# Bonus products ahead of substitution steps on VectorE, and a longer hold for the second merging product's PSUM bank in the planned TensorE order

## The chip, the cores and the metric

One core of one Trainium2 chip runs the whole program in one launch. The metric is device time in microseconds (us); lower is better. Engines are named as in the profile: PE is TensorE's matmul, PEld its weight load, DVE is VectorE, ACT is ScalarE, POOL is GpSimd, SP is the queue that issues most transfers.

## The reference, cut to what matters

One layer of a streaming encoder, for 64 frames of a running stream and 512 frames of a new one (576 tokens together), all in fp32:

```python
h = rms_norm(x, g_pre_mix)
p = h @ w_in                       # columns: r | k | v | lora_w | lora_a | lora_g | u | v_gmlp | gate_A | gate_B
# o_A, 16 heads of 64: delta-rule recurrence over the tokens, computed in chunks of 64
S = S * w_t + (S @ a_t) b_t^T + v_t k_t^T;   y_t = S @ r_t
bonus = sum_over_head(r * k_mod * r_k) * v
o_A = (group_norm(y) + bonus) * g
o_B = u * (tril(W_s) @ layer_norm(v_gmlp) + b)
m = sigmoid(gate_A) * (o_A @ w_proj_a) + sigmoid(gate_B) * (o_B @ w_proj_b)
x = x + rms_norm(m @ w_o, g_post_mix)
x = x + rms_norm((silu(f @ w_gate) * (f @ w_up)) @ w_down, g_post_ffn)      # f = rms_norm(x, g_pre_ffn)
```

Returned are both outputs, the shift rows, the recurrence states and the normalised v rows.

## The kernel before, in words

The first half of the time (to about 585 us) computes o_A for eight pairs of heads, one pair after the other, while the big projections `h @ w_in` and the weights' conversion run in between. Every fp32 weight block is split on ACT (`whi`, L302) and POOL (`wlo`, L305) and multiplied as three products; a projection block is 48 products of 128x288 into a bank of its own tag (`pj`, three banks).

For a pair p the work is cut into streams, which are Python generators:

- `elementwise(p)`: small products `z` (from the lora inputs), their tanh `sg` on ACT, a running sum `L` on DVE (L670), its exponentials `EL` (L674) and `EN` (written into `sg`, L676) on ACT, head norms `n`, then the inner products `am` into four banks, and last `bo`, the head sums of r * k * r_k, in two halves. The bonus products of the title, `bonus<-bo,v` at L790 on DVE, read the two `bo` banks and so set them free. The next pair's `elementwise` begins behind them.
- `substitute(p)`: 15 steps of forward substitution on 16x16 blocks, each an `Xt` (L863) and an `X` (L866) on DVE, 80 partitions wide. The first one is pinned behind all that was traced on DVE before it.
- `inverse(p)`: reads the substituted blocks back, and merges them into larger inverses. The first merging product (`m1`), the second (`m2`) and then `mp` and `mu` follow one another; each is many tiny products into one bank, which ACT evicts. In the trace `m1` and `m2` both appear as `m`; the eviction of the second is `IV<-m` at L903, four instructions.
- `turns(p)`: transposes `tb`, with a fifth block in a bank `tr` that three groups share. ACT copies them out to `At` and `Kt` (L818 for `tb`, L819 for `tr`), and DVE copies out the last group; TensorE may write the shared bank again only when its reader is done. POOL writes `AR<-eye` (L822) after the first group.
- `batch(p)`: products `d`, `e`, `c` and `y`; DVE adds the results of `e` and `c` into `TD` and `AR` (L972, L973); `y` takes three banks.
- `chain(p)` (products `pc`, sums `S` at L1011, then `py`) and `finish(p)` (group norm; products `to` and `g`).

All of these small products share four PSUM banks (tag `a`, `ps1`), handed out in turn.

Two mechanisms set the order of instructions. TensorE's is fixed when the program is built: the class `Weave` keeps a clock of its own (`clk.now`), adds an estimate for each matmul, and takes the first stream whose waiting time is over; while none is ready it emits the next piece of a projection. The estimates of waiting times are in the table `LAT`. Of the four banks it knows only how long each is held, which is the second argument of `ps1`:

```python
    def take(self, hold):
        self.banks.sort()
        self.banks.pop(0)
        self.banks.append(self.now + hold)

    def free(self, n=1):
        while sorted(self.banks)[n - 1] > self.now:
            yield sorted(self.banks)[n - 1] - self.now
```

A stream that needs n banks yields on `clk.free(n)`, and the clock fills the time with projections. The inner products `am` ask for four free banks. The holds are numbers in the order only: whether a bank is really free is a semaphore's matter.

The order on the other engines comes from the framework's scheduler, which plans readiness when the program is built and among ready instructions takes the one traced first; each engine then executes in that order. `tc.high_priority(HPO)` ranks an instruction as if it were traced 3000 places earlier. In the kernel before it is used for the shifted inputs (`k<-pj`, L489).

Of the kernel before, what the change touches and what calls it, by code (L numbers as in the profile page):

```python
# [8 lines left out]
ALU = mybir.AluOpType  # L9
# [8 lines left out]
HALF = T // 2  # L18
# [14 lines left out]
HPO = 3000  # L33
# [27 lines left out]
SB = 16  # L61
# [172 lines left out]
def layer(tc, I, O):  # L234
# [3 lines left out]
    pe, dve, act, pool, sp = nc.tensor, nc.vector, nc.scalar, nc.gpsimd, nc.sync  # L238
# [23 lines left out]
    def ps1(name, hold=0.0):  # L262
        clk.take(hold)
        return psum.tile([P, 512], F32, tag="a", bufs=nb["a"], name=name)
# [7 lines left out]
    def mmul(out, lhsT, rhs, **kw):  # L272
        n = 1
        for d in rhs.shape[1:]:
            n *= d
        rows = lhsT.shape[0]
        if rows != clk.rows:
            clk.now += 0.12
            clk.rows = rows
        if rhs.dtype == F32R:  # L280
            clk.now += 0.011 + n / 2400
        elif rows == P:
            clk.now += max(n, P) / 600
        else:
            clk.now += n / 2000 if rows == 64 else 0.037 if rows == 32 else 0.02
        return pe.matmul(out, lhsT, rhs, **kw)  # L286
# [210 lines left out]
    for k in range(KD):  # L497
        t = xp.tile([P, T], F32, name=f"x{k}")
# [101 lines left out]
    for k in range(KD):  # L600
        t = xp.tile([P, T], F32, tag="xsq", bufs=4, name="xn")
# [50 lines left out]
    def elementwise(E):  # L652
# [128 lines left out]
        bonus = rp2.tile([P, T], F32, tag="bonus", bufs=2, name="bonus")  # L781
        yield LAT["bo0"]
        yield (("v", hp_), LAT["v"])
        v = E["v"]
        for hs in HS:
            yield from clk.free()
            sb = ps1("bo", 2.0)
            mmul(sb[:, 0:HALF], bonesr, rkh[:, hs], start=True, stop=False)
            mmul(sb[:, 0:HALF], bonesr, rkl[:, hs], start=False, stop=True)
            dve.tensor_tensor(bonus[:, hs], sb[:, 0:HALF], v[:, hs], ALU.mult)  # L790
            yield LAT["bo"]
        E["bonus"] = bonus
        clk.signal("elem", hp_)
# [77 lines left out]
    def inverse(E):  # L871

        hp_, AB, di = E["hp"], E["AB"], d_inv[E["hp"]]
        yield LAT["O"]
        for h in range(2):
            for b in range(64 // SB):
                r0_ = 64 * h + SB * b
                sp.dma_start(IV[r0_:r0_ + SB, :, SB * b:SB * b + SB], di[1, h, b].rearrange("u s t -> s u t"))
        blocks = [(64 * h, 64 * h + 32) for h in range(2)]
        quarters = [(64 * h + 32 * b, 32 * b) for h in range(2) for b in range(2)]  # L880
        turn = lambda: dve.transpose(IT.rearrange("p c t -> p (c t)"), IV.rearrange("p c t -> p (c t)"))
        U = AB.rearrange("p j h t -> p (j h) t")
        yield lat("U", hp_)
        if hp_ > 0:
            yield (("d", hp_ - 1), 0.0)

        PT = rp.tile([P, 10, SB], F32, tag="PT16", name="PT16")
        tc.keep_in_program_order(turn())
        yield lat("m1", hp_)
        yield from clk.free()  # L890
        pp = ps1("m1", 1.8)[:, 0:10 * SB].rearrange("p (c t) -> p c t", t=SB)
        for u in range(10):
            for r, q in quarters:
                mmul(pp[r:r + 32, u], U[r:r + SB, u, q:q + 32], IT[r:r + SB, u, q:q + SB], start=True, stop=True)
        act.activation(PT, pp, ACT.Copy, scale=low)
        yield lat("m2", hp_)
        yield from clk.free()
        pp = ps1("m2", 2.2)[:, 0:10 * SB].rearrange("p (c t) -> p c t", t=SB)
        for u in range(10):
            for r, q in quarters:  # L900
                mmul(pp[r:r + SB, u], PT[r:r + 32, u, :], IV[r:r + 32, u, q + SB:q + 32], start=True, stop=True)
        for r, q in quarters:
            act.activation(IV[r:r + SB, :, q + SB:q + 32], pp[r:r + SB], ACT.Copy)  # L903

        PT = rp.tile([P, 10, 32], F32, tag="PT", name="PT")
        turn()
        yield lat("mp", hp_)
        yield from clk.free()
        pp = ps1("mp", 1.9)[:, 0:320].rearrange("p (c t) -> p c t", t=32)
        for u in range(10):  # L910
            for a0, a1 in blocks:
                mmul(pp[a1:a1 + 32, u], U[a0:a1, u, 32:64], IT[a0:a1, u, 0:32], start=True, stop=True)
        for _, a1 in blocks:
            act.activation(PT[a1:a1 + 32], pp[a1:a1 + 32], ACT.Copy)
        yield lat("mu", hp_)
        yield from clk.free()
        pp = ps1("mu", 1.9)[:, 0:320].rearrange("p (c t) -> p c t", t=32)
        for u in range(10):
            for _, a1 in blocks:
                mmul(pp[a1:a1 + 32, u], IV[a1:a1 + 32, u, 32:64], PT[a1:a1 + 32, u, :], start=True, stop=True)  # L920
        for _, a1 in blocks:
            act.activation(IT[a1:a1 + 32, :, 0:32], pp[a1:a1 + 32], ACT.Copy)
        clk.signal("it", hp_)
# [147 lines left out]
    def elem_all():  # L1071
        for p_ in range(NPAIR):
            if p_ > 0:
                yield (("elem", p_ - 1), 0.0)
            yield from elementwise(EV[p_])
        sp.dma_start(O["shift"], shc)
        yield (("values", NPAIR - 1), 0.0)
        e_es.close()
        R["g"], R["gp"] = mk("gmlp")
        R["vn"] = [slot(j) for j in range(5)]  # L1080
        clk.signal("vn")
        R["ln"] = [slot(5 + i) for i in range(2)]
        R["tril"] = R["gp"].tile([P, P], F32, name="tril")
        sp.dma_start(R["tril"], I["cst"][:, NCST:])
        for i in range(2):
            sp.dma_start(R["ln"][i][0:64], I["rows"][i:i + 1, :].broadcast_to([64, D]))
# [6 lines left out]
    def inv_all():  # L1093
        for p_ in range(NPAIR):
            yield (("x", p_), 0.0)
            yield from inverse(EV[p_])
# [465 lines left out]
```

## Time and profile before

| | us |
|---|---|
| median of 3 runs | 1229.72 (1229.62 to 1234.26) |
| the profiled execution's own time | 1231.22 |
| its span in the profile | 1229.2 |
| PE busy | 1185.0 (96%) |
| DVE busy | 548.7 (45%) |
| ACT busy | 466.8 (38%) |
| POOL busy | 603.3 (49%) |

A row of a timeline reads: start, length, engine, line, operation, output<-inputs, shapes, count; in square brackets the engine's idle time before it and who ended it. A row of waits reads: who waited, for whom, us in total, times, longest. A row of windows reads: stretch, length, then the busy time of PE, PEld, DVE, ACT and POOL with instruction counts, the granted TensorE clock (1.00 is full speed), the DMA share and GB/s.

### The profile page before, as it was taken

Reading aid. Unit: us, or ns where it says so; the run is one execution under the profiler, and the core shown is the slowest. Engines: PE = TensorE matmul, PEld = TensorE weight load, DVE = VectorE, ACT = ScalarE, POOL = GpSimd, SP = SyncE. Lnnn points to the kernel's source line nnn. Section 1 sums busy time; section 2 is a strip of 40 time slices with the busy share of each in tenths; the row PEclk is TensorE's granted clock in tenths of the full one; section 3 lists DMA queues with packets and bytes.
Section 4 is the critical chain, followed back from the end, with each engine's and each line's share of the span. In section 5 each row is a group of like instructions: output and inputs, shape, how many; then the busy total and the mean of one; then the engine's idle time right before and its main releaser. Section 6 shows DMA issues by size and latency. Waiting matters only on the chain.

```text
span 1229.2 us, 29962 instructions
## 1 busy us (share of the span) xinstructions
PE 1185.0 (96%) x12938; PEld 1152.1 (94%) x12938; DVE 548.7 (45%) x1086; ACT 466.8 (38%) x889; POOL 603.3 (49%) x477
## 2 busy tenths in 40 slices
PE   7999999999999999999999999999999999999997
PEld 6999998989888989899999999999999999999996
DVE  5756556656565656422624431754333333300103
ACT  5555544444444453343431333543222222222220
POOL 6675353535352636242545652465565555634442
PEclk9999999999999999999999999999999999999998
DMA  5233322222212222351744542232222222242222
GB/s 185 80 106 105 91 59 79 62 81 61 81 60 81 61 76 61 97 153 47 230 126 131 179 141 70 77 121 86 86 85 73 85 86 86 79 159 82 80 76 77
DMA packets 68276, 118.05 MB, mean 96 GB/s; under 512 B 30832, under 2 KB 36208, under 8 KB 68144
## 3 DMA queue, kind: packets, MB, share of 16 engines
q1 hardware_dynamic: 68000, 116.06, 30.9%
q8 instruction: 101, 1.65, 0.6%
q14 instruction: 31, 0.25, 0.1%
q10 hardware_dynamic: 144, 0.08, 0.0%
HBM read 99.83 MB, written 16.28 MB: 94 GB/s over the span
## 4 chain that ended last, share of the span: by engine, by line
PE 81%; DVE 11%; ACT 4%; issue 2%; DMA 1%; POOL 1%; POOLq 0%; ACTq 0%; DVEq 0%; SPq 0%
PE fg L286 21%; PE pj L286 17%; PE po L286 15%; PE gv L286 4%; PE pb L286 4%; PE pa L286 3%; PE fp L286 2%; PE z L286 2%; DVE X L866 1%; DVE Xt L863 1%; PE am L286 1%; PE pc L286 1%; DVE TD L972 1%; PE wv L286 1%; PE d L286 1%
## 5 line engine op out<-in xcount | busy, mean ns | idle before, releaser
L305 POOL TENSOR_TENSOR wlo<-raw,whi 128x512 fp32r<-128x512 f32 (+1 forms) x286 | 395.3, 1405 | 346.4 <-ACT whi L302 322.8
L302 ACT ACTIVATE whi<-raw 128x1024 fp32r<-128x1024 f32 x143 | 149.2, 1047 | 280.4 <-PE fg L286 174.6
L1306 DVE TENSOR_TENSOR rs<-rs,nsq 128x288 f32<-128x288 f32 (+2 forms) x12 | 9.1, 755 | 106.0 <-ACT nsq L1305 106.0
L1378 DVE TENSOR_TENSOR ft<-ft,fg 128x288 f32<-128x288 f32 x40 | 16.4, 450 | 68.2 <-PE fg L286 66.7
L1372 DVE TENSOR_TENSOR fg<-fg,rs 128x288 f32<-128x288 f32 x40 | 16.4, 452 | 63.3 <-PE fg L286 63.2
L1375 DVE SCALAR_TENSOR_TENSOR ft<-ft,fg 128x576 f32<-128x576 f32 (+1 forms) x24 | 27.9, 1163 | 18.4 <-ACT ft L1374 18.4
L1376 POOL TENSOR_TENSOR ft<-ft,rs 128x576 f32<-128x576 f32 (+1 forms) x24 | 31.9, 1327 | 6.5 <-DVE ft L1375 5.8
L1042 POOL TENSOR_TENSOR gm<-gm,mhalf 128x10 f32<-128x10 f32 x8 | 15.7, 1957 | 39.0 <-DVE gm L1041 39.0
L866 DVE TENSOR_TENSOR X<-X,Xt 80x15 f32<-80x15 f32 (+7 forms) x120 | 32.3, 269 | 3.9
L863 DVE TENSOR_TENSOR Xt<-X,M 80x15 f32<-80x15 f32 (+7 forms) x120 | 31.3, 261 | 4.9 <-DMA M<-d_inv 1.3
L822 POOL TENSOR_TENSOR AR<-eye,eC 128x576 f32<-128x576 f32 x8 | 9.4, 1177 | 47.3 <-PE tr L290 47.3
L368 POOL TENSOR_TENSOR rr<-rm,mhalf 128x3 f32<-128x3 f32 (+1 forms) x6 | 5.0, 831 | 51.9 <-DVE rm L367 51.9
L702 POOL TENSOR_TENSOR rmul<-cst,rn 128x1280 f32<-128x1280 f32 x8 | 19.0, 2379 | 22.8 <-DVE S L1011 21.0
L1011 DVE TENSOR_TENSOR S<-pc,C 128x64 f32<-128x64 f32 x48 | 10.2, 212 | 44.3 <-PE pc L286 44.3
L286 PE MATMUL pj<-h1h,whi 128*128 128x288 f32 x88 | 29.5, 336 | 0.0
L286 PE MATMUL am<-AR,BK 64*64 64x128 f32 x640 | 23.9, 276 | 4.8 <-ACT IV L903 4.8
L286 PE MATMUL pj<-h3h,whi 128*128 128x288 f32 x88 | 28.5, 324 | 0.0
L286 PE MATMUL pj<-h7h,whi 128*128 128x288 f32 x88 | 28.4, 323 | 0.0
L286 PE MATMUL pj<-h4h,whi 128*128 128x288 f32 x88 | 27.6, 313 | 0.0
L286 PE MATMUL pj<-h5h,whi 128*128 128x288 f32 x88 | 27.6, 313 | 0.0
L286 PE MATMUL pj<-h2h,whi 128*128 128x288 f32 x88 | 27.1, 308 | 0.0
L286 PE MATMUL pj<-h0h,whi 128*128 128x288 f32 x88 | 27.0, 307 | 0.0
(1200 smaller groups left out, 4304.2 us busy)
## 6 DMA issues: line engine op xcount, KB each, us to landing
raw<-in_w_in SPq DMA_DIRECT2D x50, 512.0 KB, 3.7
raw<-in_w_gate SPq DMA_DIRECT2D x22, 512.0 KB, 3.6
raw<-in_w_up SPq DMA_DIRECT2D x22, 512.0 KB, 3.6
raw<-in_w_down SPq DMA_DIRECT2D x16, 512.0 KB, 3.6
raw<-in_w_gv SPq DMA_DIRECT2D x8, 512.0 KB, 3.8
raw<-in_w_proj_a SPq DMA_DIRECT2D x8, 512.0 KB, 3.9
raw<-in_w_proj_b SPq DMA_DIRECT2D x8, 512.0 KB, 3.7
raw<-in_w_o SPq DMA_DIRECT2D x8, 512.0 KB, 3.6
```

What stands on the lines that cost most here:

```text
L286: return pe.matmul(out, lhsT, rhs, **kw)
L302: keep(act.activation(hi[:, :cols], raw[:, :cols], ACT.Copy))
L305: keep(pool.tensor_tensor(lo[:, c0:c1], raw[:, c0:c1], f(hi[:, c0:c1]), ALU.subtract))
L702: pool.tensor_tensor(rmul.rearrange("p j h t -> p (j h) t"), mask.unsqueeze(1).broadcast_to([P, 10, P]), rn.unsqueeze(2).broadcast_to([P, ...
L863: ins = dve.tensor_tensor(t3, X[:, 0:r, s:s + 1].broadcast_to([NU, r, w]), M[:, s:s + 1, s + 1:SB].broadcast_to([NU, r, w]), ALU.mult)
L866: dve.tensor_tensor(X[:, 0:r, s + 1:SB], X[:, 0:r, s + 1:SB], t3, ALU.add)
L972: dve.tensor_tensor(TD[rows, cs, rows], ps[rows, :, 1, :], by_place[rows, cs, 0, :], ALU.add)
L1042: pool.tensor_tensor(m, m, mhalf, ALU.pow)
L1372: keep(dve.tensor_tensor(g[:, HS[h]], pg, rs2[:, HS[h]], ALU.mult))
L1375: keep(dve.scalar_tensor_tensor(t[:, ts], t[:, ts], 1.0, g[:, ts], ALU.add, ALU.mult))
L1376: pool.tensor_tensor(t[:, ts], t[:, ts], rs2[:, ts], ALU.mult)
L1378: dve.tensor_tensor(t[:, HS[h]], t[:, HS[h]], pu, ALU.mult)
```

## The change

Two edits. The two bonus products of each pair are traced under high priority. The hold that the planned TensorE order counts for the bank of the second merging product goes from 2.2 to 3.4 (us of the planner's clock). No instruction is added or removed, and no operand changes.

```diff
@@ elementwise
             sb = ps1("bo", 2.0)
             mmul(sb[:, 0:HALF], bonesr, rkh[:, hs], start=True, stop=False)
             mmul(sb[:, 0:HALF], bonesr, rkl[:, hs], start=False, stop=True)
-            dve.tensor_tensor(bonus[:, hs], sb[:, 0:HALF], v[:, hs], ALU.mult)
+            with tc.high_priority(HPO):
+                dve.tensor_tensor(bonus[:, hs], sb[:, 0:HALF], v[:, hs], ALU.mult)
             yield LAT["bo"]
@@ inverse
-        pp = ps1("m2", 2.2)[:, 0:10 * SB].rearrange("p (c t) -> p c t", t=SB)
+        pp = ps1("m2", 3.4)[:, 0:10 * SB].rearrange("p (c t) -> p c t", t=SB)
         for u in range(10):
             for r, q in quarters:
                 mmul(pp[r:r + SB, u], PT[r:r + 32, u, :], IV[r:r + 32, u, q + SB:q + 32], start=True, stop=True)
```

## The prediction

> **What bounds the kernel now.** I read the page first, then TensorE's waits, then the timeline around the longest ones, then the granted clock by windows.
>
> ```profile
> PE 1185.0 (96%) x12938; PEld 1152.1 (94%) x12938; DVE 548.7 (45%) x1086; ACT 466.8 (38%) x889; POOL 603.3 (49%) x477
> ...
> PE y L286 <- DVE bonus L790: 11.9, 6, 2.3
> PE am L286 <- ACT IV L903: 4.8, 6, 1.1
> ...
> PE tr L290 <- ACT Kt L819: 0.3, 1, 0.3
> ```
>
> TensorE is busy for 96% of the span, and neither edit removes work from it. So the change can only take idle time away, or time at a reduced clock. The other rows are waits of TensorE between 100 and 600 us, the two largest and a small one: six times `y` waits for a bonus product, six times `am` for the eviction L903, once a third transpose for `Kt`. I number the passes 2 to 7 by the pair whose `bo` and X steps run there; `y` then belongs to the pair before.
>
> A wait can cost more than itself:
>
> ```profile
> 213.30:216.70 3.40, 1.77 (x14) 1.53 (x13) 1.17 (x1) 2.14 (x7) 0.20 (x1) 1.00 0.14 29
> 216.70:220.10 3.40, 3.15 (x26) 2.91 (x25) 1.76 (x5) 3.40 (x7) 2.25 (x2) 1.00 0.27 27
> 267.90:271.30 3.40, 3.40 (x55) 3.28 (x48) 2.99 (x15) 1.61 (x6) 0.00 (x0) 0.50 0.39 153
> ...
> 387.30:390.70 3.40, 1.55 (x57) 1.48 (x58) 3.23 (x10) 0.32 (x2) 1.36 (x2) 1.00 0.30 60
> 390.70:394.10 3.40, 3.40 (x15) 3.40 (x15) 2.95 (x15) 2.03 (x8) 0.00 (x0) 0.51 0.24 96
> ...
> 448.70:452.10 3.40, 2.40 (x64) 2.34 (x65) 3.09 (x14) 1.17 (x6) 0.25 (x1) 1.00 0.53 159
> ...
> 510.20:513.60 3.40, 3.40 (x15) 3.40 (x16) 2.50 (x13) 0.99 (x4) 0.00 (x0) 0.50 0.20 81
> ```
>
> After a stretch of 3.4 us with PE busy for 1.55 us (387.30, pass 5), the next 3.4 us are granted half the clock, which costs 1.7 us of work; after 1.77 us busy (213.30, pass 2) they are not. A half-clock stretch followed the `y` wait in four passes, 3, 4, 5 and 7, the first at 267.90 and the last at 510.20; pass 6's wait escaped (448.70). Together the `y` waits cost 11.9 + 4 x 1.7 = 18.7 us. The question is how much of that comes back.
>
> **The change, part by part. The bonus products.** Pass 4, with the end of its stream on each engine:
>
> ```profile
> 320.95 0.85 DVE L972 TENSOR_TENSOR TD<-e,AR 64x256 f32<-64x256 f32 x2
> 322.76 0.16 DVE L863 TENSOR_TENSOR Xt<-X,M 80x15 f32<-80x15 f32 x1
> 323.91 0.29 PE L286 MATMUL bo<-rkl,bonesr 128*128 128x288 f32 x1
> 327.43 0.45 DVE L790 TENSOR_TENSOR bonus<-bo,v 128x288 f32<-128x288 f32 x1
> 327.94 0.55 PE L286 MATMUL y<-Vt,AK 64*64 64x64 f32 x10 [2.28 <-DVE bonus L790]
> 332.14 0.18 DVE L866 TENSOR_TENSOR X<-X,Xt 80x15 f32<-80x15 f32 x1
> 337.03 0.27 PE L290 MATMUL tr<-cst,BK 128*128 128x128 f32 x1
> 354.78 0.84 DVE L881 STREAM_TRANSPOSE IT<-IV 128x640 f32<-128x640 f32 x1 [0.15 <-issue]
> ```
>
> The product at 327.43 stands behind twelve X operations, though both halves of `bo` are done by 324.20. Ranked ahead, it runs about 3.5 us earlier, before `y` needs its bank at 325.66 (327.94 less 2.28). The wait goes. No instruction is added: the two products (0.45 us each) stood inside the X chain anyway, so its end at 332.32 stays. Even later it would not matter for the blocks' way back, which DVE takes up at 354.78. SP's queue keeps its order, and neither product issues a transfer. A product put ahead of an unfinished `bo` would idle DVE: none of that at best; at worst both ahead of the first X, which is 0.9 us per pass net (below, fourth rival). I take none, because `bo`'s first half is done when X begins.
>
> What is late next: the second `tr`, which needs `At` copied out (L819). ACT does that behind `EL` (L674), `EL` needs `L`, and `L` stands behind the X steps on DVE. Pass 2 shows it, because its `y` wait was only 0.78 us:
>
> ```profile
> 202.50 0.16 DVE L863 TENSOR_TENSOR Xt<-X,M 80x15 f32<-80x15 f32 x1
> 206.18 0.55 PE L286 MATMUL y<-Vt,AK 64*64 64x64 f32 x10 [0.78 <-DVE bonus L790]
> 212.02 1.15 POOL L822 TENSOR_TENSOR AR<-eye,eC 128x576 f32<-128x576 f32 x1 [6.54 <-PE tr L290]
> 212.17 1.04 DVE L866 TENSOR_TENSOR X<-X,Xt 80x15 f32<-80x15 f32 x1
> 213.12 1.34 DVE L670 TENSOR_TENSOR_SCAN L<-rmask,sg 128x576 f32<-128x576 f32 x1
> 214.56 0.69 ACT L674 ACTIVATE EL<-L 128x576 f32<-128x576 f32 x1 [2.09 <-DVE L L670]
> 215.15 0.26 ACT L819 ACTIVATE At<-tr 128x128 f32<-128x128 f32 x1
> 215.46 0.33 PE L290 MATMUL tr<-cst,BK 128*128 128x128 f32 x1 [1.63 <-ACT At L819]
> ```
>
> From the first X to the second `tr` pass 2 took 12.96 us, bound by DVE and ACT all along: no gap on DVE before `L`, TensorE waiting at the end. That includes an X step stretched from 0.18 to 1.04 us beside POOL's L822, which in passes 3 to 6 fell after X (TensorE was late) and will fall into it once TensorE is early. So 12.96 us is my floor for passes 2 to 6. What they take now:
>
> ```profile
> 262.22 0.16 DVE L863 TENSOR_TENSOR Xt<-X,M 80x15 f32<-80x15 f32 x1
> 276.39 0.27 PE L290 MATMUL tr<-cst,BK 128*128 128x128 f32 x1
> ...
> 384.22 0.16 DVE L863 TENSOR_TENSOR Xt<-X,M 80x15 f32<-80x15 f32 x1
> 398.17 0.27 PE L290 MATMUL tr<-cst,BK 128*128 128x128 f32 x1
> ...
> 444.52 0.16 DVE L863 TENSOR_TENSOR Xt<-X,M 80x15 f32<-80x15 f32 x1
> 457.16 0.27 PE L290 MATMUL tr<-cst,BK 128*128 128x128 f32 x1
> ```
>
> Pass 3: 14.17; pass 4: 337.03 - 322.76 = 14.27; pass 5: 13.95; pass 6: 12.64. Against the floor that is -1.2, -1.3, -1.0, +0.3, and nothing for pass 2 (its 0.78 us moves to the `tr` wait): -3.2 us. Pass 7 has no `L` behind its X, and `y` is TensorE's only wait there, so it gets all back: -2.3 - 1.7 = -4.0.
>
> The new `tr` waits are long. Pass 2: 1.63 + 0.78 = 2.4. Pass 4: 12.96 - (14.27 - 2.28 - 1.7) = 2.7; 3 and 5 alike. Pass 6: 12.96 - (12.64 - 2.3) = 2.6. By the windows above a wait lowers the clock if about 1.75 us of it falls into one window; for 2.6 us that holds for (1.65 + 0.85) / 3.4 = 0.74 of the positions. The wait of pass 6 that escaped makes me take a little less, 3 of 5 passes: +5.1 us. Bounds: 0 and +8.5.
>
> **The longer hold.**
>
> ```profile
> 360.46 0.82 PE L286 MATMUL m<-IV,PT 32*16 32x16 f32 x80
> 362.19 1.30 PE L286 MATMUL am<-AR,BK 64*64 64x128 f32 x34
> 363.34 1.20 ACT L903 ACTIVATE IV<-m 16x160 f32<-16x160 f32 x4
> 364.59 0.68 PE L286 MATMUL am<-AR,BK 64*64 64x128 f32 x14 [1.10 <-ACT IV L903]
> ```
>
> This is the longest of the six. The bank of `m2` is taken at 360.46 and free at 364.54: 4.1 us, where the order counts 2.2. With 3.4 the order puts 1.2 us more of projections ahead of `am`; it starts at 363.4, its first part needs 1.3 us, and the rest meets a free bank. `am` ends where it did (363.4 + 2.0 against 365.27), so what it feeds, the eight transfers on SP included, does not move on the chip. The projections are done earlier instead of later, at no cost while others are left. Term: -4.8, bounds 0 and -4.8.
>
> The cover for that is the stretch behind the last `py`:
>
> ```profile
> 584.97 0.34 PE L286 MATMUL py<-S,AR 64*64 64x64 f32 x8
> 613.73 0.74 DVE L347 TENSOR_TENSOR m7l<-xt,m7h 128x576 fp32r<-128x576 f32 x1
> 631.87 0.43 PE L286 MATMUL pa<-m7h,whi 128*128 128x288 f32 x2
> ```
>
> The last pair's result is ready (`m7l`, 614.47) 29.5 us after `py`, and TensorE first uses it 46.9 us after. Eight passes that each draw 1.2 us of projections forward shorten that by 9.6 us; 7.8 us are left, so I cost it at nothing. With the cover gone each further us would be one of waiting.
>
> Behind the second `tr` pass 2 also has the small wait of the third for `Kt` (0.3 us in the waits, the only one). It should come to four more passes; I take 0.25 each: +1.0.
>
> Sum: -4.8 - 4.0 - 3.2 + 1.0 + 5.1 = -5.9 us. The profiled execution took 1231.22 us, 1.5 above the median; I take the difference off the median: 1223.8, say 1224 (a profiled execution of 1225.3).
>
> **The rivals.** First, ACT copies `At` ahead of `EL`, so that no `tr` wait follows: all waits and all half-clock stretches go, -4.8 - 18.7 = -23.5, or 1206. For it: the scheduler's plan sees TensorE earlier. Against: in pass 2, with TensorE early, L674 still stands ahead of L819.
>
> Second, the `tr` waits come but leave the clock alone: -11.0, or 1219. For it: pass 2's window with 1.77 us busy, behind a wait of 1.63. Against: the window with 1.55, and waits that are longer. [...]
>
> Third, the priority moves nothing, because the products become ready late in the plan: only the second edit acts, -4.8, or 1225. Against: twelve X operations are passed over with `bo` done.
>
> Fourth, and slower: the products are planned ahead of DVE's sums too, and DVE stands idle for `bo`. If both were ahead of X only, X would start at 324.2 + 0.45 instead of 322.76, 1.9 later, with 0.9 saved inside the chain: 1.0 per pass, five passes, and the gain is just gone. Ahead of the sums from 320.95 on, their 1.9 us come on top: 2.9 x 5 = 14.5, so +8.6, or 1238. It decides from 2.4 us per pass, (5.9 + 6.1) / 5. Against: the product has only `bo` to wait for, and the scheduler ranks it only once it expects `bo` done.
>
> **How the numbers follow.** About 0.5%, 6 us, is what a measurement of this kernel can tell from no change, so "faster" means below 1223.6. My forecast has 0.46, with a range of its own from 1219 to 1228 (two to five half-clock stretches, a floor off by 0.5 us per pass); the rivals have 0.12, 0.20, 0.09 and 0.13. Faster: 0.12 + 0.19 + 0.4 x 0.46 = 0.49. Slower: 0.11, most of the fourth. Same: the rest, 0.40. The range 1206 to 1232 leaves out about half of the first rival and most of the fourth, under 2 in 10.
>
> **What would show it.** Right: no `y` wait on `bonus`, no `am` wait on L903, products right behind `bo` on DVE; in five passes a `tr` wait of 2.4 to 2.8 us on L819, 12.9 to 13.1 us after the first X, half clock after about three of them; pass 7 shorter by 4 us. Wrong: L819 ahead of L674 (first rival), DVE idle for `bo` (fourth), or new waits at `mp`, `gv` or `pa`, since the projections' order moves as a whole.

## The result, and the profile after

The changed kernel took 1248.73 us (median of four runs, 1242.86 to 1251.72), the kernel before on the same chip 1230.03 (1229.62 to 1234.26). The ratio is 1.0138 with a 95% interval of 1.0095 to 1.0182: slower by 1.4%, or 18.7 us by the medians. The forecast was 1224, and its range ended at 1232.

TensorE's waits after (who waited, for whom, us in total, times, longest):

```profile
PE d L286 <- DVE oo L1063: 17.1, 5, 4.6
PE pc L286 <- DVE S L1012: 5.8, 4, 2.0
PE pc L286 <- DVE So L1012: 5.5, 3, 1.8
PE pa L286 <- ACT s L448: 1.9, 1, 1.9
PE y L286 <- DVE bonus L791: 0.2, 1, 0.2
```

Both waits that the forecast wanted gone are gone: `y` for the bonus product fell from 11.9 to 0.2 us, and `am` for the eviction (L903 before, L904 after, where the new line moves the rest down by one) is no longer in the list. In their place stands one that the forecast does not name, 17.1 us at `d` for the product `oo<-oo,g` on VectorE, and 11.3 us at the chain's `pc`. Waits changed by 17.1 + 11.3 - 11.9 - 4.8 = +11.7 us.

The summary of the bonus sums' second products, first for the kernel before, then after, and behind each the first part of the projection through `w_proj_a` (count, shortest/median/longest ns, first and last start in us):

```profile
L286 PE MATMUL bo<-rkl,bonesr x16: 292/294/297, 89.8 to 504.7; 128*128 128x288 f32 x16
L286 PE MATMUL pa<-m0h,whi x16: 293/295/399, 615.1 to 669.1; 128*128 128x288 f32 x16
```

```profile
L286 PE MATMUL bo<-rkl,bonesr x16: 291/296/445, 90.2 to 522.9; 128*128 128x288 f32 x16
L286 PE MATMUL pa<-m0h,whi x16: 293/295/422, 633.8 to 689.4; 128*128 128x288 f32 x16
```

The first `bo` falls at the same time, the last 18.2 us later (504.7 to 522.9), and `pa` begins 18.7 us later. So the whole loss has arisen by the last `bo`, that is in passes 2 to 7, and the stretch behind it is as long as it was. In that stretch the `y` wait and the half clock of pass 7 are gone (4.0 us by the forecast's reading), but `pa` waits 1.9 us where it waited 0.5, and 3.4 us from 617.0 on are granted half the clock (0.51 from 616.9 to 620.3). Windows over most of those passes, before and then after (stretch, length, busy time of PE, PEld, DVE, ACT and POOL with counts, granted clock, DMA share, GB/s):

```profile
200.00:530.00 330.00, 311.44 (x4985) 294.14 (x4976) 199.12 (x477) 150.37 (x345) 142.77 (x114) 0.98 0.26 74
```

```profile
200.00:530.00 330.00, 300.78 (x4834) 283.32 (x4833) 189.96 (x471) 142.85 (x329) 140.99 (x110) 0.96 0.25 69
```

TensorE is idle for 10.7 us more, and the clock is lower by 0.02, which is 6.6 us of 330. Together 17.3 us, near the 18.2. In that stretch eight slots of 3.4 us were granted half the clock (0.50 or 0.51, from 258.6, 262.0, 292.7, 326.8, 347.3, 391.7, 456.6 and 477.1), four before (from 267.8, 329.3, 390.7 and 510.2): 4 x 1.7 = 6.8 us.

Pass 5 of the changed kernel shows the new wait (timeline: start, length, engine, line, operation, in brackets the idle time before it and who ended it; `M` in a row is the tile that the first X step reads, brought by a transfer):

```profile
381.17 0.33 SPq L856 DMA_DIRECT2D M<-d_inv  x1
...
384.14 0.17 DVE L864 TENSOR_TENSOR Xt<-X,M 80x15 f32<-80x15 f32 x1 [5.92 <-DMA M<-d_inv]
384.51 0.29 PE L286 MATMUL g<-dgh,lgl 128*128 128x288 f32 x1
385.54 1.17 PE L286 MATMUL d<-AB,IT 64*64 64x128 f32 x32
388.99 0.75 DVE L1056 TENSOR_TENSOR oo<-oo,bonus 128x576 f32<-128x576 f32 x1
390.81 0.44 DVE L1063 TENSOR_TENSOR oo<-oo,g 128x288 f32<-128x288 f32 x1
391.31 0.75 PE L286 MATMUL d<-AB,IT 64*64 64x128 f32 x4 [4.60 <-DVE oo L1063]
395.55 0.46 DVE L791 TENSOR_TENSOR bonus<-bo,v 128x288 f32<-128x288 f32 x1 [1.12 <-PE bo L286]
```

VectorE reaches the first X step 5.92 us before the transfer of `M` has landed, and everything behind that step waits with it: first the sum `oo<-oo,bonus`, then the products `oo<-oo,g` that free the banks of `g`. TensorE finished `g` by 384.8 and then multiplied 32 of the 36 parts of `d`; the last four need a third bank, `g`'s, and start only at 391.31. In the same pass of the kernel before VectorE did these things in another order:

```profile
374.98 0.76 DVE L1055 TENSOR_TENSOR oo<-oo,bonus 128x576 f32<-128x576 f32 x1 [2.48 <-ACT oo L1053]
378.20 0.46 DVE L1062 TENSOR_TENSOR oo<-oo,g 128x288 f32<-128x288 f32 x1 [2.46 <-PE g L286]
381.20 0.86 DVE L972 TENSOR_TENSOR TD<-e,AR 64x256 f32<-64x256 f32 x2 [1.76 <-PE e L286]
384.22 0.16 DVE L863 TENSOR_TENSOR Xt<-X,M 80x15 f32<-80x15 f32 x1
388.65 0.44 DVE L790 TENSOR_TENSOR bonus<-bo,v 128x288 f32<-128x288 f32 x1
```

There `oo`, then `TD`, then X, and the bonus product within X. After, the bonus product stands behind X, yet not because of a rank: its `bo` is issued only at 395.03. X itself begins at 384.2 in both, but the changed kernel is 8.5 us behind by then (the `py` of this pass starts at 364.82, not 356.34), so X has moved that much nearer to `py` and in front of work that stood ahead of it. VectorE's waits for `M` in the changed kernel (the kernel before has 1.3 us, once):

```profile
DVE Xt L864 <- DMA M<-d_inv: 24.3, 6, 5.9
```

### The profile page after: what moved, and what is told of

It is laid out like the page before. It is cut to its first block, busy times and chain, and to the rows that moved or that the text cites. A ratio compares the mean times of both kernels' runs of the same rounds, so it can differ in the third digit from the quotient of the medians.

```text
span 1241.1 us, 29948 instructions
## 1 busy us (share of the span) xinstructions
PE 1183.5 (95%) x12938; PEld 1150.2 (93%) x12938; DVE 538.1 (43%) x1086; ACT 466.5 (38%) x889; POOL 606.4 (49%) x477
## 4 chain that ended last, share of the span: by engine, by line
PE 70%; DVE 15%; ACT 6%; DMA 4%; issue 2%; SPq 2%; POOL 1%; ACTq 0%; DVEq 0%; POOLq 0%
PE fg L286 20%; PE po L286 14%; PE pj L286 12%; PE pb L286 4%; PE gv L286 3%; PE pa L286 3%; PE fp L286 2%; SPq L750 2%; DVE Xt L864 1%; DMA M<-d_inv 1%; DVE X L867 1%; PE z L286 1%; DMA d_inv<-AB 1%; PE wv L286 1%; PE pc L286 1%
## 5 line engine op out<-in xcount | busy, mean ns | idle before, releaser
L305 POOL TENSOR_TENSOR wlo<-raw,whi 128x512 fp32r<-128x512 f32 (+1 forms) x286 | 399.1, 1418 | 393.0 <-ACT whi L302 381.4
L286 PE MATMUL pc<-S,TD 128*128 128x64 f32 x112 | 20.2, 262 | 11.3 <-DVE S L1012 5.8
L286 PE MATMUL d<-AB,IT 64*64 64x128 f32 x288 | 14.5, 282 | 17.1 <-DVE oo L1063 17.1
L286 PEld LDWEIGHTS pc<-S,TD 128*128 128x128 f32 x112 | 17.7, 191 | 12.5 <-DVE S L1012 6.8
L286 PEld LDWEIGHTS d<-AB,IT 64*64 64x64 f32 x288 | 11.0, 133 | 19.6 <-DVE oo L1063 18.3
L286 PE MATMUL pj<-h6h,whi 128*128 128x288 f32 x88 | 27.9, 316 | 0.0
```

Source lines behind the costliest of these rows:

```text
L305: keep(pool.tensor_tensor(lo[:, c0:c1], raw[:, c0:c1], f(hi[:, c0:c1]), ALU.subtract))
```

## The experiments

Two theories stood at the start: that the `y` wait turned into the `tr` wait of the forecast and more, or that the longer hold re-threads TensorE's order. Each experiment was timed beside runs of the kernel before on the same chip. Most expectations set two theories of their own against each other; "theory one" and "theory two" below are those of the expectation just above.

**The first edit alone.**

```diff
-            dve.tensor_tensor(bonus[:, hs], sb[:, 0:HALF], v[:, hs], ALU.mult)
+            with tc.high_priority(HPO):
+                dve.tensor_tensor(bonus[:, hs], sb[:, 0:HALF], v[:, hs], ALU.mult)
```

> Only the first edit: the bonus products under high priority, the hold at 2.2. Theory: the scheduler places a product when its plan has bo done, and the plan has that late, so rank changes nothing. Then the time is that of before (1230, within 0.2%), the y waits on L790 stay at about 12 us in six, and the products stand behind ten to twelve X operations as before. Rival: the rank moves the products; then there are no y waits and the time is between 1206 and 1226, or, if early products block VectorE, above 1236.

Measured: 1227.17 us, ratio 0.9991 (0.996 to 1.0022).

```profile
PE y L286 <- DVE bonus L790: 11.9, 6, 2.3
```

The wait is what it was, to the tenth. The order of instructions is that of the kernel before on all five engines: the priority moves nothing.

**The second edit alone.**

```diff
-        pp = ps1("m2", 2.2)[:, 0:10 * SB].rearrange("p (c t) -> p c t", t=SB)
+        pp = ps1("m2", 3.4)[:, 0:10 * SB].rearrange("p (c t) -> p c t", t=SB)
```

> Only the second edit: the hold at 3.4, no priority. Theory: this alone makes the slowdown, 1243 to 1252, with d waiting five times, 17 us together, for the products oo<-oo,g (L1062) that stand behind X steps on VectorE. Rival: both edits are needed; then less than half of the 18 us, below 1239.

Measured: 1248.34 us, ratio 1.0172 (1.0125 to 1.022), with the changed kernel's order on every engine and its waits:

```profile
PE d L286 <- DVE oo L1062: 17.2, 5, 4.4
```

So the whole effect is the hold's, and the `y` wait goes with it: it is 0.2 us here too, with no priority on the bonus products. The order in a middle pass of the traces, first TensorE's (numbers are projection products between):

```
before: py m1 18 m2  6 am 21 mp 3 am 3 mu 3 to 6 to 6 d 6 g 3 g 9 e c 12 bo 6 bo 6 y z
after:  py 9 m1 12 am 21 m2 am 24 mp to 3 to 9 mu 6 g 6 d 12 bo 6 bo 6 z 6 e c ... y
VectorE before: AB AK oo+ oo* oo* TD AR TD AR TD AR X11 bonus X2 bonus X17 L
VectorE after:  AB AK X12 oo+ X5 oo* X oo* X12 bonus bonus TD AR TD AR TD AR L
```

(`oo+` is L1055, `oo*` L1062, X12 twelve instructions of the substitution.) In the first pass the hold delays `am` by nine projections; `to` and `g`, whose stream does not wait for `am`, then come earlier relative to it, and from the next pass on `am` of a pair overtakes `m2` of the pair before. The inverse and `d` come later behind `py`, `g` stands before `d`, `y` starts 8.4 us behind the last `bo` (404.67 after 396.27) where 1.0 us lay between, and X, whose place follows from `am` through the planner's delay `M`, stands in front of `oo` and `TD`.

**ScalarE copies the bonus bank out, GpSimd multiplies** (hold 2.2), to test the floor at the second `tr`.

```diff
-            dve.tensor_tensor(bonus[:, hs], sb[:, 0:HALF], v[:, hs], ALU.mult)
+            act.activation(bonus[:, hs], sb[:, 0:HALF], ACT.Copy)
+            pool.tensor_tensor(bonus[:, hs], bonus[:, hs], v[:, hs], ALU.mult)
```

> The hold stays at 2.2 and TensorE's order is that of before. ScalarE copies each half of bo out of its bank and GpSimd multiplies it by v, so the bank no longer waits for VectorE's X steps. This gives what the first edit was to give. Theory (the prediction's floor): the y waits go, but a tr wait of 2.4 to 2.8 us on L819 takes their place in passes 2 to 6, and only pass 7 gets all back: 1222 to 1230. Rival: nothing is late next, all 18.7 us come back: about 1211.

Measured: 1238.53 us, ratio 1.0096 (1.0064 to 1.0127).

```profile
PE tr L290 <- ACT At L819: 18.0, 5, 3.6
```

```profile
400.69 0.21 DVE L863 TENSOR_TENSOR Xt<-X,M 80x55 f32<-80x55 f32 x1
400.94 1.27 DVE L866 TENSOR_TENSOR X<-X,Xt 80x55 f32<-80x55 f32 x1
```

The `y` wait became a `tr` wait, longer than forecast: X steps that take 0.2 us took 0.73 and 0.74 beside GpSimd's bonus products, and X ran 11.1 us in this pass against 9.6 before. The 1.27 us of the step shown are not the edit's: it stands beside GpSimd's weight conversion (L305, from 400.86), which the kernel before has there too. A single wait of 4.6 us at `tv` and one of 2.2 at `e` came on top. That left open how much of the `tr` wait was the floor's.

**The same with VectorE multiplying the copy**, so that GpSimd does nothing more.

```diff
-            dve.tensor_tensor(bonus[:, hs], sb[:, 0:HALF], v[:, hs], ALU.mult)
+            act.activation(bonus[:, hs], sb[:, 0:HALF], ACT.Copy)
+            dve.tensor_tensor(bonus[:, hs], bonus[:, hs], v[:, hs], ALU.mult)
```

> The kernel before, except that ScalarE copies the bonus product's bank to the tile bonus and VectorE then multiplies that by v in place: y's bank comes free without VectorE, the order on TensorE is that of before, and GpSimd gets no extra work beside X. Theory one (the floor of 12.96 us from the first step of X to the second tr, through the wait for At's copy, stands behind the y wait): y waits 0 to 1 us, tr waits of 2.0 to 3.0 us in five passes, 10 to 15 us in all, half clock behind each as before behind y, 1222 to 1232. Theory two (the tr wait of 3.6 us in the version with GpSimd came from GpSimd's products beside X alone): tr waits under 1 us each, 12 us of wait and some 7 us of half clock go, 1206 to 1214.

Measured: 1230.05 us, ratio 1.0000 (0.9978 to 1.0022).

```profile
PE tr L290 <- ACT At L819: 15.5, 5, 3.2
...
385.61 0.16 DVE L863 TENSOR_TENSOR Xt<-X,M 80x15 f32<-80x15 f32 x1
396.54 1.34 DVE L670 TENSOR_TENSOR_SCAN L<-rmask,sg 128x576 f32<-128x576 f32 x1
397.98 0.69 ACT L674 ACTIVATE EL<-L 128x576 f32<-128x576 f32 x1 [3.62 <-DVE L L670]
398.57 0.26 ACT L819 ACTIVATE At<-tr 128x128 f32<-128x128 f32 x1
398.88 0.33 PE L290 MATMUL tr<-cst,BK 128*128 128x128 f32 x1 [3.16 <-ACT At L819]
```

Here the forecast's first step really happens: `y` waits for nothing. The second `tr` starts 13.27 us after the first X step (12.95 in pass 2), with L, EL and the copy of `At` in a row before it. Theory one holds, with waits a little over its 2.0 to 3.0: 11.9 us of waits at `y` went, and those at `tr` for `At` rose from 1.6 to 15.5, at no change of the time.

**`am` kept behind `m2` of the pair before, the planner's clock set back by 1.2 us**, and 1.2 us of projections put there (hold 2.2).

```diff
+        if hp_ > 1: yield (("m2", hp_ - 1), 0.0)         # elementwise, ahead of am
         yield from clk.free(4)
+        if hp_ > 1: yield 1.2; clk.now -= 1.2
...
+        clk.signal("m2", hp_)                            # inverse, behind the eviction of m2
```

> The hold stays at 2.2. From pair 2 on, am waits until the second merging product of the pair before has been issued, then 1.2 us of projections go ahead of it, and the planner's clock is set back by 1.2, so that the other streams keep their distance. Theory: the slowdown comes from the new interleaving (am ahead of m2, g ahead of d), not from the longer pause: the am waits (4.8 us) go, most passes have no d wait, and the time is 1222 to 1231. Rival: drawing projections forward costs by itself (weights or the pc chain late): 1238 or more.

Measured: 1236.71 us, ratio 1.0098 (1.0059 to 1.0136). Waits at `am`, `d` and nearly `y` are gone, but the order became irregular from pass 3 on:

```profile
PE m L286 <- DVE IT L883: 3.8, 1, 3.8
```

That is the longest of many single waits that took the place of two regular ones; neither theory foresaw them, and the time lies between the two forecasts. The run tells only how easily the order changes.

**A third of the longer hold**, 2.6.

```diff
-        pp = ps1("m2", 2.2)[:, 0:10 * SB].rearrange("p (c t) -> p c t", t=SB)
+        pp = ps1("m2", 2.6)[:, 0:10 * SB].rearrange("p (c t) -> p c t", t=SB)
```

> The hold of the second merging product 2.6 in place of 2.2 (3.4 in the changed kernel), and nothing else. Theory one (the cost is in the order: from 2.6 on the planner puts am ahead of m2, the inverse later and g six products ahead of d, as with 3.4): d waits of 3 us or more in four or five passes, 1238 to 1252, the whole of the changed kernel's loss with a third of its hold. Theory two (the cost grows with the hold, 0.4 of 1.2 us): 1.0172 becomes about 1.006, 1230 to 1236, and am waits go from 4.9 to about 2.

Measured: 1241.89 us, ratio 1.0100 (1.0041 to 1.016).

```profile
PE d L286 <- DVE oo L1062: 26.9, 5, 7.1
```

The order has turned already, and the waits are theory one's: 26.9 us at `d`, more than with 3.4. The time is less clear, as the interval holds the prices of both theories.

**`am` behind `m2`, hold 3.4**: `am` of a pair waits in the plan for `m2` of the pair before.

```diff
+        if hp_ > 1: yield (("m2", hp_ - 1), 0.0)         # elementwise, ahead of am
...
+        clk.signal("m2", hp_)                            # inverse, behind the eviction of m2
```

> Hold 3.4 as in the changed kernel, and am of a pair may not be placed before m2 of the pair before it: the order is m1, 18 projections, m2, 15 projections, am, so that nothing overtakes, while g still stands only three to six projection products ahead of d. Theory one (g close ahead of d is what costs): d waits of 3 us or more in three to five passes stay, the am waits are gone, 1238 to 1252. Theory two (am ahead of m2 is what costs, it delays the inverse): no d waits over 1 us, 1224 to 1233.

Measured: 1231.07 us, ratio 0.9998 (0.9973 to 1.0023).

```profile
PE n L286 <- ACT Y L995: 6.9, 3, 2.5
...
378.79 0.85 DVE L1064 TENSOR_TENSOR oo<-oo,g 128x288 f32<-128x288 f32 x2 [1.60 <-PE g L286]
387.91 0.16 DVE L864 TENSOR_TENSOR Xt<-X,M 80x15 f32<-80x15 f32 x1
```

No `d` waits, though `g` is as close ahead of `d`. So closeness alone is not the cause, as theory one had it: X stands nine microseconds behind `oo` here, and VectorE does not wait for `M`. Without the overtaking, X does not come in front.

**The overtaking kept, `g` far ahead of `d`**: hold 3.4, and 4.0 for `g`, which puts 27 projections between the two.

```diff
-            ps = ps1("g", 1.4)
+            ps = ps1("g", 4.0)
```

> Hold of the second merging product 3.4 as in the changed kernel, and the hold of the gate's product g 1.4 -> 4.0, so that in the order 27 projection products (3.6 us) stand between g and d, not six (0.8 us). Theory one (what the longer hold costs is d: its third bank is g's, g's product with oo stands on VectorE behind the substitution X, and TensorE waits 17.1 us at d in five passes, with four stretches of half clock behind them, 17 us at half speed = 8.5 us): the d waits shrink to under 4 us in all, and the time comes to 1223 to 1233, at most 0.5% above before. Theory two (the time is lost because the inverse stands later in the order, and X and what follows it are on the path anyway): the wait turns up at e, c or y instead, with 15 us or more, and the time stays at 1242 to 1252.

Measured: 1227.56 us, ratio 0.9969 (0.9943 to 0.9996).

```profile
PE d L286 <- DVE oo L1062: 5.3, 4, 2.1
...
379.51 0.17 DVE L863 TENSOR_TENSOR Xt<-X,M 80x15 f32<-80x15 f32 x1 [6.24 <-DMA M<-d_inv]
386.18 0.44 DVE L1062 TENSOR_TENSOR oo<-oo,g 128x288 f32<-128x288 f32 x1
386.68 0.75 PE L286 MATMUL d<-AB,IT 64*64 64x128 f32 x4 [2.12 <-DVE oo L1062]
```

Theory one, though its bound of 4 us was passed by 1.3. VectorE still stands 6.24 us at `M` with `oo` behind, but TensorE multiplies projections meanwhile, and the loss is gone. So the loss was in the waits that go here, and not in a later inverse by itself. Most of it is `d`'s, 17.2 to 5.3 us, but the chain's `pc` waits fell as well, from 11.3 to 3.9; behind them lay three of the eight stretches of half clock in the changed kernel (from 292.7, 347.3 and 477.1). Why `pc` waits there stays open: in the version with hold 2.6, which has the overtaking too, it does not.

**X later on VectorE.** Hold 3.4, and the planner's delay `M` 11 to 14; then the same with `g` at 4.0.

```diff
-    "M": 11.0, "X": 0.65, ...
+    "M": 14.0, "X": 0.65, ...
```

> Hold 3.4 as in the changed kernel, and the planner's delay M (from the products am to the substitution X) 11 -> 14 us, so that on VectorE the two products oo<-oo,g and the bonus products are issued ahead of X's first step, which waits for the transfer of M. TensorE's order of the changed kernel stays from py to d: m1, 12 and 21 projections with am between, m2, ..., g, six projections, d. Theory one (the loss is VectorE's order: X's first step, issued early, stands up to 5.9 us at M's transfer, oo behind it, and d behind oo): no VectorE wait on M above 1 us, d waits under 3 us in all, 1222 to 1234. Theory two (TensorE's order with am ahead of m2 loses the time by itself, through a later inverse): the wait moves to e, c, y or pc, and the time stays at 1238 or above.

> As e9_mlate, and g's hold 1.4 -> 4.0, which alone gave 0.9969 beside hold 3.4: 27 projections between g and d, and X behind the products oo and bonus. Theory one (the waits left in that version, d 5.3 us, bo 2.4 us behind oo, z 1.5 us behind bonus, are VectorE's order too): these 9 us go, and the two stretches of half clock behind them (3.4 us of loss), against new waits at n or e of 3 us at most: 1216 to 1226, a ratio of 0.985 to 0.997. Theory two (nothing more is to be had there: what TensorE no longer waits for at d it waits for at pc, n or e, since X begins later and the next pair's chain with it): 1224 to 1234, the ratio of that version or above.

Measured: 1251.88 us, ratio 1.0196 (1.0155 to 1.0236), and 1233.89 us, 1.0044 (1.0015 to 1.0072). Both are misses for theory one, and the first took a time that theory two gives. In the first, VectorE's wait for `M` is 1.0 us and none is left at `d`, as it said; but the time did not come back:

```profile
PE n L286 <- ACT Y L993: 8.2, 5, 2.8
PE y L286 <- ACT C L976: 5.9, 5, 1.6
PE tr L290 <- ACT Kt L819: 3.8, 1, 3.8
PE z L286 <- DVE X L866: 3.1, 4, 0.8
```

X had moved behind `oo` and the bonus products, but in front of `TD`, and `n`, `y`, `tr` and `z` waited in `d`'s place. With `g` at 4.0 as well the time is theory two's, but the largest wait is 8.8 us at `y`, where it had named `pc`, `n` or `e` (3.4 at `pc`, 2.2 at `n`).

**X last.** Hold 3.4, `M` 17, `n2` 11.2: VectorE's order is `oo`, bonus, `TD`, then X.

```diff
-    "z0": 5.4, "z": 0.85, "n2": 8.2, ...
+    "z0": 5.4, "z": 0.85, "n2": 11.2, ...
-    "M": 11.0, "X": 0.65, ...
+    "M": 17, "X": 0.65, ...
```

> Hold 3.4 as in the changed kernel, the planner's delay M 11 -> 17 us and its delay n2 8.2 -> 11.2 us. TensorE's order still has am ahead of m2 from py to mu; VectorE's has X behind the products oo, the bonus products and the sums TD and AR out of e, with L after X's 12th instruction; n stands 18 projections behind z, not nine. In the version with M 14 X stood ahead of TD, and TensorE waited for z, y and n instead of d (17 us in all), with half clock behind. Theory one (X's ten microseconds on VectorE, placed ahead of something that TensorE needs soon, are the loss, whatever that something is: bonus before, oo in the changed kernel, TD with M 14): with X behind all of them no wait over 1 us at d, z, y or n in passes 3 to 6, fewer than five stretches of half clock between 250 and 550 us, 1218 to 1231. Theory two (am ahead of m2 loses the time by itself, since the inverse comes later): new waits at m1, e or tr, or projections that run out, and 1238 or above.

Measured: 1235.93 us, ratio 1.0087 (1.0059 to 1.0116), between the two theories.

```profile
PE pc L286 <- DVE So L1011: 10.9, 5, 2.3
PE to L290 <- DVE Y L1044: 7.0, 1, 7.0
```

The waits at `d`, `z`, `y` are under 1 us, as theory one said, and at `n` up to 1.2, but the chain's `pc` waits up to 2.3 us a pass, and behind the last pair TensorE waits 7.0 us for the group norm. That fits pairs that end late because X is late; no run separates it. Theory two as it stands is not borne out either: the version with `g` at 4.0 has `am` ahead of `m2` and loses nothing.

**The hold of `g` alone**: the last diff of `g`, with `m2` at 2.2.

> The kernel before with g's hold 1.4 -> 4.0 alone; the hold of the second merging product stays at 2.2. In the order am now overtakes m2, and 27 projections stand between g and d, as in the version with both holds. Theory one (the distance from g to d decides what the re-threaded order costs, and the hold of m2 matters only as one way to turn the order): the time of the version with both holds, 1220 to 1231, a ratio of 0.993 to 1.001, and no am waits although m2's hold is unchanged. Theory two (the hold of m2 itself helps there, by the am waits of 4.8 us): am waits of 4 to 5 us are back, and the ratio is 0.4% higher, 1.000 to 1.006.

Measured: 1223.21 us, ratio 0.9952 (0.9932 to 0.9971): the version that beats both kernels, by 0.5% against the kernel before.

```profile
PE d L286 <- DVE oo L1062: 5.7, 5, 2.2
...
200.00:530.00 330.00, 318.24 (x5243) 299.30 (x5242) 197.46 (x487) 153.94 (x350) 152.38 (x119) 0.99 0.28 81
```

The `am` waits are down to 0.6 us with `m2`'s hold untouched, so the number that was to remove them is not needed for it: the first 48 products of `am` stand ahead of `m2` here too. From 200 to 530 us the granted clock is 0.99 and TensorE is busy for 318.24 us, against 0.98 and 311.44 in the kernel before, and the last `bo` falls at 496.9, 7.8 us before that of the kernel before.

## Why the prediction was wrong, point by point

**"Ranked ahead, it runs about 3.5 us earlier": failed.** The terms -4.0, -3.2, +1.0 and +5.1, -1.1 us in all, rested on a move that does not take place. The third rival, given 0.09, was true of this edit (its -4.8 for the other was not). Its argument against, that twelve X operations are passed over with `bo` done, reads the trace's readiness; the order is made from the plan's, and there the rank decided nothing. That the products were not yet ready in the plan fits, but no run shows the plan. The sign "no `y` wait on `bonus`" came true by luck: the hold's new order took the wait away, in the version without the priority as well.

**"`am` ends where it did, so what it feeds does not move on the chip": failed, and it is the step that cost the range.** The term was -4.8 us. The `am` waits did go (4.8 us), yet only in the first pass because `am` starts later behind `m2`: from there on the hold moved `am` past `m2`, `g` past `d`, and X past `oo` and `TD`. The step treated a hold as a delay of one product, with the order otherwise kept; it is an input to every later choice of the planner, whose state carries over from pass to pass. The cost was +11.7 us of waits net of those removed, and +6.8 us of half clock.

**"New waits at `mp`, `gv` or `pa`, since the projections' order moves as a whole":** the right worry in the wrong place. `pa` waits 1.9 us (0.5 before) and `gv` 2.3 (1.2 before), `mp` 0.5 as before; `d` and `pc` have 28.4. The order did not move as a whole, it was re-threaded. The cover behind the last `py`, 46.9 - 29.5 = 17.4 us in the forecast, was not the issue, as the stretch behind the last `bo` kept its length.

**The floor of 12.96 us: right, but not reached by the change.** With `y` freed by ScalarE it was 12.95 in pass 2 and 13.27 in pass 5, and the `tr` waits were 2.8 to 3.2 us against 2.4 to 2.8 forecast. The forecast's own terms for that edit, -1.1 us, meet the measured ratio of 1.0000, and not only in the sum: in pass 7 the first transpose follows the last `bo` 4.2 us sooner than before (4.0 forecast), and the clock fell behind a `tr` wait too. In pass 5 the products of 128x288 start 0.24 us apart behind the wait of 3.16 us (398.97 to 401.62), 0.13 us apart ahead of it; in the kernel before they start 0.24 us apart where the granted clock was 0.51 (from 390.98). From 200 to 530 us the clock granted in that version is 0.98, as before. By an estimate from this rounded figure (0.975 to 0.985 over 330 us) 5 to 8 us are lost, or three to four half-clock slots of 1.7 us each (three forecast). The third transpose's wait for `Kt` did not spread to more passes; the +1.0 for it was too much.

**The clock: right in kind.** Windows of the changed kernel around a `pc` wait (columns as above):

```profile
289.30:292.70 3.40, 1.37 (x11) 1.13 (x10) 2.87 (x5) 1.51 (x5) 2.64 (x2) 1.00 0.25 58
292.70:296.10 3.40, 3.40 (x45) 3.00 (x44) 0.19 (x1) 0.77 (x2) 0.44 (x1) 0.50 0.25 96
```

Here a stretch with 1.37 us busy was followed by one granted 0.50, and the longest wait ahead of it, `pc`'s, was 2.0 us; in the kernel before 0.51 followed the 1.55 us at 387.30. The forecast's 1.75 us of a wait in one window was an estimate from two rows, with 1.55 and 1.77 us busy. The bound that it drew between them is not sharp: in the changed kernel a stretch with 1.87 us busy (from 453.16) was followed by half clock (0.50 from 456.56), and one with 1.73 (from 514.60) was not (1.00 from 518.00). The second rival, `tr` waits that leave the clock alone, is refuted by pass 5 of the version in which ScalarE copies and VectorE multiplies, above.

**The first and fourth rivals** needed products that move, and none did. With ScalarE copying the bonus bank, `EL` still stands ahead of the copy of `At`, against the first. The time fell beyond the fourth's 1238 by another way.

## What to carry to other kernels

A number in a planner (a hold, a delay, a priority) is not a local edit: compare the built order on every engine before pricing it, and price the differences found there, of which one edit here had none and the other changed every pass. A long serial block on one engine, here VectorE's substitution that begins at a transfer and took 9.6 us in pass 4 of the kernel before (322.76 to 332.32), made someone wait wherever it stood in these versions (bonus, `oo`, `TD`, `EL`, the chain); what paid was to leave the block in front and give TensorE other work, 27 projections, between the producer of a bank and the product that needs it next. A wait that is removed should be followed to the next one in the row before it is counted.

## What the runs showed of the hardware

The `fg` products, late in the program and in the same order in all versions, run at one of two paces. First and last start of one of their groups, in the kernel before and in the changed one:

```profile
L286 PE MATMUL fg<-f0h,whi x80: 292/295/399, 818.2 to 1069.0; 128*128 128x288 f32 x80
```

```profile
L286 PE MATMUL fg<-f0h,whi x80: 291/292/398, 837.0 to 1081.6; 128*128 128x288 f32 x80
```

That is 250.8 and 244.6 us, both at a granted clock of 1.00 (windows 818 to 950 and 950 to 1080). The kernel with the second edit alone, whose order is the changed kernel's, took the slower pace (835.1 to 1085.8 in its own summary), so the 6.2 us do not come from the order of instructions. They fit the changed kernel's profiled execution, 1242.86, which lies 5.9 us below its median, and they are as large as some of the differences above. The version with the hold of `g` alone keeps its gain at the same pace: its profiled execution took 1221.71 us with 250.7 us for this group, the kernel before 1231.22 with 250.8. What sets the pace stays open.
